# A decoder block's front half on one core: 64-row score blocks with a separate diagonal, a written order that reaches to the first pair's preparation, and the gate vector summed in idle buffers

## The chip, the core and the metric

The kernel runs on one core of a Trainium2 chip. The metric is the device time of one execution in microseconds (us). Times come from repeated executions, of which the median counts; the profile is of one further execution, with its own time.

## What is computed

A decoder block for 512 tokens of width 1024, depth 1. Window attention (8 heads of 64, window 128) and gated linear attention (4 heads, 64 keys by 128 values) share one input projection; the block ends with a layer of experts. Cut to what the change touches:

```python
mod = jax.nn.silu(c) @ w_ada[l] + b_ada[l]
shift1, scale1, gate1, shift2, scale2, gate2 = jnp.split(mod[:, None, :], 6, axis=-1)
h = rms_norm(x, norm1_w[l]) * (1.0 + scale1) + shift1
proj = h @ w_in[l]
aq, ak, av, gq, gk, gv, gg, glr = jnp.split(proj, split_points, axis=-1)
...
b = jnp.cumsum(gt, axis=2)
...
decay = jnp.exp(jnp.where(causal[:, :, None], diff, -jnp.inf))
att = jnp.einsum('bhtd,bhsd,bhtsd->bhts', qt, kt, decay)
...
mixed = jnp.concatenate([att, go], axis=-1) @ w_out[l]
x = x + gate1 * mixed
```

## The kernel before, in words

The tokens are four tiles of 128. The first fifth of the run, called the front half here, ends with the output projection and the second norm; after it comes the expert layer, which this change does not touch.

The front half has three stretches. **The quarter stage** (lines 354 to 443) runs in a fixed written order for all engines (`tc.manual_schedule`). The shift and scale vectors of the first norm are sums over `w_mod` weights, which DVE makes quarter by quarter (`quarter_sum`, L269 and L271); PE turns a quarter's sum into columns (`quarter_columns`, L278), DVE adds the bias (`quarter_rows`, L282 and L283), ACT writes two rows k of the normed input in a high part (`h_row`, L312) and DVE its low part (`h_low`, L317). Each k then feeds products into five PSUM banks at once (`first_products`, run at L348): the low-rank gate (`pglr`) and the column groups 3 and 4 of `w_in` (the queries and keys of the linear attention). Every matmul of the projections is three: high by high, high by low, low by high. The weights of groups 3 and 4 are split into a high part by ACT (L327) and a low part by GpSimd (L328), in halves `w3,0`, `w3,1`, `w4,0`, `w4,1`; the high and low parts live in rings of three buffers each, so `w4,1` takes the buffer of `w3,0`, which the products of k 0 to 3 read.

**The projections 0 to 2** (L70 to L72 into tiles named `pj`) follow: attention queries, keys, values. Beside them DVE and ACT work out the decays (`decays`) and the preparation of the first pair of token tiles (`gla_prep(0)`): prefix sums, eight differences `Eg[L]`, one absolute value over seven of them (L582) and one exponential over eight (L583) on ACT, and 14 products with q and k (L588, L589) plus one (L593) on DVE.

**The attention stretch** is all that follows up to the output projection `pw`: scores of the linear attention for four tiles (`gla_scores`, into PSUM `pa`), window attention for four tiles (`attention`: `sc`, the softmax on DVE and ACT in tiles `sS`, transposes `pt`, products `po`), the second pair's preparation, the value and gate projections 5 to 8 (`proj_N`, tiles `pn`), and the vectors 2, 3 and 4 of the modulation (`mod_part`): each loads eight 128x1024 blocks of `w_ada` (two per 1 MB transfer `wa`, L214) and sums them on DVE (`macc`, L218 and L220). These transfers share a ring of three 1 MB buffers ("raw") with the projections' weights (`wi`, L247) and the output projection's (`wo`, L770). Vector 2 is the gate `gate1b`; it is spread over the partitions by two matmuls with ones (L227, tiles `gb`) and added to its bias (L228). In this stretch the order on each engine is made by a scheduler from a model of the times, with the source order as the start.

`gla_scores` cuts the causal 128x128 block of a tile into levels: level 0 is the lower half by the upper half (L611), level 1 two 32x32 pieces (L614), levels 2 to 6 are made 32 rows at a time (L627, 32x16 each, of which a mask keeps a part, L634), and the block diagonal of 32x32 is a product of k and q without decay (L630, mask L637). That is 4 + 8 + 80 + 16 matmuls for a tile. ACT then copies the pieces into the tile `at` (three copies and four).

## Time and profile before

| | us |
|---|---|
| median of 3 runs | 1479.56 (1479.05 to 1480.74) |
| the profiled execution's own time | 1479.41 |
| its span | 1477.6 |
| busy in the span: PE / DVE / ACT / GpSimd | 1428.0 / 1279.9 / 680.3 / 557.5 |
| quarter stage ends, projections 0 to 2 end | 62.5, 97.7 |
| first matmul of the output projection | 228.3 |

All starts are counted from the start of the span. PE is TensorE, PEld its weight loads, DVE VectorE, ACT ScalarE, POOL GpSimd, SP the engine that issues most DMAs. A row of a timeline gives start, duration, engine, line, operation, output<-inputs, shape, count, and in brackets how long the engine was idle before it and who released it ("issue": nothing the profile shows). A row of the windows gives the stretch, its length, then for each engine the busy time and in parentheses the number of instructions, then the mean TensorE clock granted (1.00 is full), the share of the DMA engines and their rate. A matmul of plain fp32 (scores, transposes, sums) stands in the records as two, one of the projections' format (fp32r) as one.

### The profile page before, as it was taken

To read this page: it belongs to the slowest core of one execution; us is meant where nothing else is said; L and a number is where in the kernel's file an instruction comes from. 1 tells how busy PE (TensorE), PEld (TensorE's weight loads), DVE (VectorE), ACT (ScalarE), POOL (GpSimd) and SP (SyncE) were. 2 spreads that over 40 slices of the span, in tenths; PEclk is the share of its full clock that TensorE was granted. 3 is DMA by queue.
4 is the path that set the end of the run, shared out by engine and by line. 5 is a ranking of instruction groups with operands and counts; after the bars stand their busy time and mean duration, and the time that the engine had idled before them with its cause. 6 is when DMAs were issued, how large, how long until landed. Compare 5 with 4: busy or idle time off the path is not lost.

```text
span 1477.6 us, 24740 instructions
## 1 busy us (share of the span) xinstructions
PE 1428.0 (97%) x9427; PEld 1269.7 (86%) x9427; DVE 1279.9 (87%) x2475; ACT 680.3 (46%) x1073; POOL 557.5 (38%) x386
## 2 busy tenths in 40 slices
PE   4989899999999999999999999999999999999997
PEld 3778587788899999999999888888888888888886
DVE  7487647859999899999886998999999989999997
ACT  4545366643343365555765334333333334333334
POOL 4000000034441344421023666666666666544520
PEclk9999699999999999999999999999999999999999
DMA  9252605535246889997789999999999999999972
GB/s 358 102 187 90 224 30 199 177 126 205 73 156 228 321 301 343 338 364 267 255 292 383 414 412 414 412 414 402 383 405 394 398 405 410 410 411 413 410 301 72
DMA packets 130072, 439.57 MB, mean 297 GB/s; under 512 B 13328, under 2 KB 49440, under 8 KB 109600
## 3 DMA queue, kind: packets, MB, share of 16 engines
q1 hardware_dynamic: 71728, 258.42, 46.1%
q0 software_dynamic: 44832, 163.60, 28.5%
q10 hardware_dynamic: 13392, 15.97, 3.0%
q8 instruction: 74, 1.21, 0.3%
q14 instruction: 46, 0.38, 0.1%
HBM read 393.36 MB, written 44.52 MB: 296 GB/s over the span
## 4 chain that ended last, share of the span: by engine, by line
PE 82%; DVE 8%; DMA 4%; issue 3%; ACT 2%; POOL 0%; SPq 0%; ACTq 0%; DVEq 0%; POOLq 0%
PE acc L72 12%; PE acc L70 12%; PE acc L71 11%; PE ph L70 9%; PE ph L72 9%; PE ph L71 9%; PE pg L1080 4%; DMA Gd<-gs 1%; DMA wa<-in_w_ada_dram 1%; PE pj L348 1%; PE pn L70 1%; PE sc L526 1%; PE pn L71 1%; PE pn L72 1%; PE pw L71 1%
## 5 line engine op out<-in xcount | busy, mean ns | idle before, releaser
L1207 POOL DMA_INDIRECT gu<-in_u_dram,ix_u x128 | 194.4, 1519 | 193.6 <-PE pg L1080 77.8
L1242 POOL DMA_INDIRECT gv<-in_vP_dram,ix_v x128 | 196.8, 1537 | 155.0 <-DVE gu L1217 54.5
L841 ACT ACTIVATE ge<-ph 128x336 f32<-128x336 f32 x128 | 57.7, 451 | 309.2 <-PE ph L72 306.5
L1247 DVE SCALAR_TENSOR_TENSOR gacc<-gv,hg,gacc 128x1024 f32<-128x1024 f32 x127 | 162.2, 1277 | 5.0 <-DMA gv<-in_vP_dram,ix_v 4.7
L1217 DVE SCALAR_TENSOR_TENSOR gu<-gu,h2n 128x1024 f32<-128x1024 f32 x128 | 155.2, 1216 | 3.2 <-DMA gu<-in_u_dram,ix_u 3.1
L1155 POOL DMA_INDIRECT spr<-in_u_dram,spix x48 | 81.7, 1702 | 164.7 <-DVE spr L1161 124.1
L1525 ACT ACTIVATE Ah<-gr 128x384 fp32r<-128x384 f32 x128 | 66.6, 520 | 104.5 <-DVE gr L1522 104.0
L1301 POOL IOTA iot<- 128x256 bf16 x1 | 1.5, 1536 | 257.8 <-DVE h2Tl L816 257.8
L1082 ACT ACTIVATE gs<-pg 128x512 f32<-128x512 f32 x96 | 95.5, 1109 | 2.2 <-PE pg L1080 2.2
L1073 DVE TENSOR_TENSOR o<-o,gp 128x3072 bf16<-128x3072 bf16 x48 | 84.0, 1750 | 5.3 <-PE pg L1080 5.2
L1537 DVE TENSOR_TENSOR Al<-gr,Ah 128x384 fp32r<-128x384 f32 x128 | 70.3, 549 | 4.8 <-DMA Gd<-gs 4.8
L1080 PE MATMUL pg<-o,o 128*128 128x128 bf16 x1152 | 74.1, 219 | 0.0
L1080 PEld LDWEIGHTS <-o 128*128 128x128 bf16 x1152 | 66.9, 97 | 4.6
L1161 DVE SCALAR_TENSOR_TENSOR spr<-spr,xs 128x1024 f32<-128x1024 f32 x48 | 58.4, 1217 | 10.7 <-DMA spr<-in_u_dram,spix 10.7
L1055 DVE TENSOR_TENSOR o<-iot,t 128x2048 bf16<-128x2048 bf16 x48 | 58.2, 1218 | 6.0 <-PE pg L1080 4.1
L220 DVE SCALAR_TENSOR_TENSOR macc<-wa,scs,macc 128x1024 f32<-128x1024 f32 x28 | 38.4, 1372 | 5.0 <-DMA wa<-in_w_ada_dram 4.7
L1522 DVE TENSOR_TENSOR gr<-gel,gr 128x336 f32<-128x336 f32 x64 | 32.0, 501 | 0.0
L71 PE MATMUL pq<-h2Tl,wq_0h 128*128 128x512 f32 (+1 forms) x80 | 27.9, 349 | 1.2 <-DVE h2Tl L816 1.2
L70 PE MATMUL pq<-h2Th,wq_0h 128*128 128x512 f32 (+1 forms) x80 | 28.0, 352 | 1.0 <-ACT qsc L907 1.0
L72 PE MATMUL pq<-h2Th,wq_1l 128*128 128x512 f32 (+1 forms) x80 | 28.2, 353 | 0.0
L71 PE MATMUL pq<-h2Tl,wq_1h 128*128 128x512 f32 (+1 forms) x80 | 28.0, 350 | 0.0
L70 PE MATMUL pq<-h2Th,wq_1h 128*128 128x512 f32 (+1 forms) x80 | 27.9, 349 | 0.0
(2590 smaller groups left out, 5039.0 us busy)
## 6 DMA issues: line engine op xcount, KB each, us to landing
u<-in_uT_dram SPq DMA_DIRECT2D x64, 1024.0 KB
v<-in_vP_dram SPq DMA_DIRECT2D x64, 1024.0 KB
gr<-Gd SPq DMA_DIRECT2D x15, 1536.0 KB
Gd<-gs SPq DMA_DIRECT2D x10, 2048.0 KB
wa<-in_w_ada_dram SPq DMA_DIRECT2D x16, 1024.0 KB
gsp<-ge ACTq DMA_DIRECT2D x88, 168.0 KB
gel<-gsp SPq DMA_DIRECT2D x32, 336.0 KB
wo<-in_w_out_dram SPq DMA_DIRECT2D x8, 1024.0 KB
```

The costliest lines, as they stand in the source:

```text
L70: nc.tensor.matmul(acc, lh, rh, start=start, stop=False)
L71: nc.tensor.matmul(acc, lh, rl, start=False, stop=False)
L72: return nc.tensor.matmul(acc, ll, rh, start=False, stop=stop)
L1073: nc.vector.tensor_tensor(o2, o12[:, :, 1, None].to_broadcast([P, H, 3, P, 2]), gp3[:, g0:g0 + H, :, None].to_broadcast([P, H, 3, P, 2]), ...
L1080: nc.tensor.matmul(pt[:, i, :], o12[:, g, 0, :, r], o2[:, g, m, :, r], start=(m == 0), stop=(m == 2))
L1082: evict = nc.scalar.activation(gs[:, :, q % 2, :, t0 + 4 * f:t0 + 4 * f + 4].rearrange("p c i a -> p a c i"), pt.rearrange("p a (c i) -> p ...
L1155: nc.gpsimd.indirect_dma_start(out=sp[m], out_offset=None, in_=a["u"], in_offset=bass.IndirectOffsetOnAxis(ap=sp["ix", i][:, j:j + 1], axi ...
L1207: nc.gpsimd.indirect_dma_start(out=ur, out_offset=None, in_=a["u"], in_offset=bass.IndirectOffsetOnAxis(ap=ix_u[:, s:s + 1], axis=0))
L1217: nc.vector.scalar_tensor_tensor(ur, ur, 1.0, h2n, op0=OP.mult, op1=OP.mult, accum_out=hid[:, s:s + 1])
L1242: nc.gpsimd.indirect_dma_start(out=vr, out_offset=None, in_=a["vP"], in_offset=bass.IndirectOffsetOnAxis(ap=ix_v[:, s:s + 1], axis=0))
L1247: nc.vector.scalar_tensor_tensor(gacc, vr, hg[:, s:s + 1], gacc, op0=OP.mult, op1=OP.add)
L1537: nc.vector.tensor_tensor(grp(Al), A, grp(Ah), OP.subtract)
```

## The change

It has three parts.

1. *Scores.* Levels 1 to 6 are each made in two blocks of 64 rows (4 heads each, stationary 64x64, 32 columns), with level 0 as before: 52 matmuls for a tile. The diagonal is separate: GpSimd multiplies q by k into `Eg[NL + 1]`, PE sums it over the 64 rows of a head with a selection matrix `sel` (four matmuls into `pd` for a pair of tiles), DVE copies it out. The masked copies on DVE are six of 128x128 and one of 128x256 for a tile; ACT copies level 0 and two 64-row blocks.
2. *Written order.* The fixed order now reaches from the first quarter to the transposes of the values after projection 2; the decays, the projections 0 to 2 and the first pair's preparation are spelled out in it. Inside the quarter stage, the low parts of groups 3 and 4 move from GpSimd to DVE, the second half of group 3 is loaded behind the third quarter's weights, and group 4's products are run quarter by quarter instead of being kept for k 0 to 3 in one run behind `xt2`.
3. *Gate vector.* Its eight weight blocks are loaded one by one into tiles that are idle then (the softmax tiles, parts of `Eg` and `qT`), issued behind the weights of group 0, and summed on DVE at the end of the quarter stage and in projection 0; its two matmuls stand ahead of projection 1. The parts 3 and 4 stand in the source behind `proj_N(8)`.

The diff, cut to its core:

```diff
+    def mod_loads(k0, k1):
+        for k in range(k0, k1):
+            if k < 2:
+                home = frT.tile([P, 4, 256], F32, tag="sS", bufs=2, name=f"wm{k}")
+            else:
+                home = (Eg[:, 4:6, :], Eg[:, 7:9, :], qT[:, 0:2, :], qT[:, 2:4, :], Eg[:, 0:2, :], Eg[:, 2:4, :])[k - 2]
+            gate_in[k] = home.rearrange("p a b -> p (a b)")
+            nc.sync.dma_start(gate_in[k], a["w_ada"][k * P:(k + 1) * P, :D])
+
+    def mod_sums(k0, k1):
+        if k0 == 0:
+            gate_in["acc"] = frA.tile([P, D], F32, tag="m4", bufs=2, name="macc_g")
+        for k in range(k0, k1):
+            mod_sum(gate_in["acc"], gate_in.pop(k), k)
...
+    def prep_ends(i):
...
+        nc.vector.tensor_tensor(qe, Eg[:, NL + 1, :], q, OP.mult)
+        nc.vector.tensor_copy(el, grp(Eg[:, NL + 1, :], P)[:, :, P - 1])
+        nc.gpsimd.tensor_tensor(Eg[:, NL + 1, :], q, k, OP.mult)
...
+    def diagonal(i):
+        pb = bank(f"pd{i}")
+        for n in range(2):
+            for j in range(2):
+                nc.tensor.matmul(pb[:, 4 * n:4 * n + 4].rearrange("p (s j) -> p s j", j=2)[:, :, j],
+                                 Eg[:, NL + 1, n * 256 + j * P:n * 256 + (j + 1) * P], sel, start=True, stop=True)
+        pd = frG.tile([P, 2, 4], F32, tag="pd", bufs=2, name=f"pd{i}")
+        nc.vector.tensor_copy(pd.rearrange("p n h -> p (n h)"), pb[:, 0:8])
+        return pd
...
-    def w_split(g, s):
+    def w_high(g, s):
+        nc.scalar.activation(w34[g, s][0], wraw["wi", g][:, 4 * s:4 * s + 4, :], AF.Copy)
+
+    def w_low(g, s):
         h, l = w34[g, s]
-        w = wraw["wi", g][:, 4 * s:4 * s + 4, :]
-        nc.scalar.activation(h, w, AF.Copy)
-        nc.gpsimd.tensor_tensor(l, w, h, OP.subtract)
+        nc.vector.tensor_tensor(l, wraw["wi", g][:, 4 * s:4 * s + 4, :], h, OP.subtract)
 
...
         quarter_load(2)
+        w_load(3, 1)
         w_load(4, 1)
         nc.scalar.activation(wgh, wg, AF.Copy)
...
+            if q == 0:
+                nc.vector.tensor_tensor(wgl, wg, wgh, OP.subtract)
+                w_low(3, 0)
             quarter_rows(q)
-            if q == 1:
-                h_row(k0)
-                w_split(4, 0)
-                h_row(k1)
-            else:
-                h_row(k0)
-                h_row(k1)
+            if q == 3:
+                del mtb
+            h_row(k0)
+            h_row(k1)
             if q == 0:
-                w_split(3, 1)
-            j0, j1 = (first_products(k, [A] + B3 + (B4 if q > 1 else [])) for k in (k0, k1))
+                w_high(4, 0)
+            elif q == 1:
+                w_high(3, 1)
             if nxt < 4:
                 quarter_sum(nxt, (1, 2))
             h_low(k0)
             if nxt < 4:
                 quarter_sum(nxt, (3, 4))
             h_low(k1)
+            if q < 2:
+                w_low(*((4, 0), (3, 1))[q])
+            elif q == 3:
+                w_high(0, 0)
+                w_low(0, 0)
+                mod_sums(0, 2)
...
-            run(j0)
             if q == 0:
+                run(first_products(k0, [A] + B3))
                 xt_part(1, range(NT))
-                run(j1[:3])
+                run(first_products(k1, [A] + B3))
+                run(first_products(k0, B4))
                 quarter_columns(1)
-                run(j1[3:])
+                run(first_products(k1, B4))
...
-            elif q == 1:
-                run(j1)
+                continue
+            run(first_products(k0, [A] + B3 + B4))
+            if nxt < 4:
+                xt_part(nxt, range(NT))
+            jobs = first_products(k1, [A] + B3 + B4)
+            run(jobs[:6])
+            if nxt < 4:
+                quarter_columns(nxt)
+            run(jobs[6:])
+            jobs = None
+            if q == 1:
...
                 w_alloc(4, 1)
-                w_split(4, 1)
-                xt_part(2, range(NT))
-                for k in range(4):
-                    ops = B4
-                    run(first_products(k, ops))
-                    if k == 0:
-                        quarter_columns(2)
-                w34.pop((4, 0))
+                w_high(4, 1)
+                w_low(4, 1)
+                wraw.pop(("wi", 3))
+                mod_loads(0, 4)
+                fetch(a["w_in"][1], 1, 256, "wi")
+                mod_loads(4, 6)
...
+                wraw.pop(("wi", 4))
+                mod_loads(6, KD)
+                fetch(a["w_in"][2], 2, 256, "wi")
+                bcast_load(ba_tile(), a["b_ada"][0:1, 2 * D:3 * D], D)
...
+        w_high(0, 1)
+        mod_sums(2, 4)
+        w_low(0, 1)
+        mod_sums(4, 6)
+        pz = bank("pz0")
+        z_product(0, pz)
+        evict(p3.pop(), halves_of(gq, 1), 0.125)
+        pj = pbank("pj00")
+        group_products(0, 0, pj)
+        z_chain(0, pz)
+        evict(p3.pop(), halves_of(gq, 0), 0.125)
+        mod_sums(6, KD)
+        evict(pj, qT[:, 0, :], 0.125)
+        pz = bank("pz1")
+        z_product(1, pz)
+        pj = pbank("pj01")
+        group_products(0, 1, pj)
...
+        gate_products()
+        evict(pj, qT[:, 1, :], 0.125)
+        pj = pbank("pj10")
+        group_products(1, 0, pj)
+        prep_diffs(0)
+        gate_adds()
+        w_alloc(2, 0)
...
-        for L in (*LW, NL):
-            m = 64 >> L
-            for b0 in (0, 64):
+        for L in LW:
+            lo = 64 + (L - 1) * 32
+            for B in (0, 64):
                 for j, s, r, c in heads:
-                    for b in (b0, b0 + 32):
-                        cb = slice(c + b, c + b + 32)
-                        if L < NL:
-                            lo = 96 + (L - 2) * 16
-                            nc.tensor.matmul(pa[b:b + 32, 2 * s + j, lo:lo + 16], E[r, L, cb], late(E[r, L, cb], m),
-                                             start=True, stop=True)
-                        else:
-                            nc.tensor.matmul(pa[b:b + 32, 2 * s + j, 176:208], k[r, cb], q[r, cb], start=True, stop=True)
+                    cb = slice(c + B, c + B + 64)
+                    nc.tensor.matmul(pa[B:B + 64, 2 * s + j, lo:lo + 32], E[r, L, cb], late(E[r, L, cb], 64 >> L),
+                                     start=True, stop=True)
+        if n % 2 == 0:
...
+        nc.vector.copy_predicated(tc64, lm[:, NL - 1, :].bitcast(U16)[:, None].to_broadcast([P, 4, 64]),
+                                  pd[:, n % 2, :][:, :, None].to_broadcast([P, 4, 64]))
+        for b in (0, 64):
+            nc.scalar.activation(at[b:b + 64, :, b:b + 64], tc64[b:b + 64], AF.Copy)
...
     proj_N(5, gv, 0)
-    mod_part(2, frA, "m4", 2, dst=gate1b)
     attention(1)
     proj_N(6, gv, 256)
-    mod_part(3, frA, "m4", 2)
     gla_scores(2)
     gla_state(0, False)
     attention(2)
     gla_scores(3)
     gla_state(1, False)
     proj_N(7, gg, 0)
-    mod_part(4, frA, "m4", 2)
     attention(3)
     proj_N(8, gg, 256)
+    mod_part(3, frA, "m4", 2)
+    mod_part(4, frA, "m4", 2)
```

What moves on the engines follows in pieces of the instruction order. Line numbers are those of each kernel's own file; a number behind a name tells tiles of one name apart.

On ACT, at the turn from the second to the third quarter (`hTh`/`h32` are the rows from `xt1` and `xt2`, `wi3_1hi` and so on the high parts), before:

```order
L327 ACTIVATE wi4_0hi_281<-wi4_208 128x1024
L312 ACTIVATE hTh_182<-xt1_324,modT_83,aT_84 128x512
L312 ACTIVATE h32_3_368<-xt1_324,modT_83,aT_84 128x512
L327 ACTIVATE wi4_1hi_398<-wi4_208 128x1024
L312 ACTIVATE hTh_182<-xt2_402,modT_83,aT_84 128x512
```

and now:

```order
L429 ACTIVATE hTh_186<-xt1_328,modT_83,aT_84 128x512
L429 ACTIVATE h32_3_382<-xt1_328,modT_83,aT_84 128x512
L442 ACTIVATE wi3_1hi_284<-wi3_201 128x1024
L442 ACTIVATE wi4_1hi_439<-wi4_211 128x1024
L429 ACTIVATE hTh_186<-xt2_411,modT_83,aT_84 128x512
```

The high part of `w4,1` stands right ahead of the first row from `xt2` in both; the high part of `w3,1` has come in ahead of it, that of `w4,0` has left.

On DVE at the same place (`macc2`, `macc3` are the sums of the third and fourth quarter; `modT` and `aT` are what `h_row` of `xt2` reads), before:

```order
L271 SCALAR_TENSOR_TENSOR macc2_359<-mixA3_117,scs_85,macc2_359 128x512
L269 TENSOR_SCALAR macc3_439<-la0_103,scs_85 128x512
L282 TENSOR_TENSOR modT_83<-mt_187,vec_69 128x2x2
L283 SCALAR_TENSOR_TENSOR aT_84<-modT_83,vec_69 128x2
L271 SCALAR_TENSOR_TENSOR macc3_439<-gq0_104,scs_85,macc3_439 128x512
```

and now:

```order
L388 SCALAR_TENSOR_TENSOR macc2_375<-mixA3_117,scs_85,macc2_375 128x512
L446 TENSOR_TENSOR wi4_1lo_440<-wi4_211,wi4_1hi_439 128x1024
L386 TENSOR_SCALAR macc3_453<-la0_103,scs_85 128x512
L399 TENSOR_TENSOR modT_83<-mt_191,vec_69 128x2x2
L400 SCALAR_TENSOR_TENSOR aT_84<-modT_83,vec_69 128x2
L388 SCALAR_TENSOR_TENSOR macc3_453<-gq0_104,scs_85,macc3_453 128x512
```

The low part of `w4,1` now stands on DVE between the last sum of the third quarter and the rows `modT` and `aT`; before, it was on GpSimd.

On DVE in the attention stretch, around the masked copies of the third tile's scores (`macc4` and `macc3` are the sums of vectors 4 and 3, `wa4_4` and so on their transfers of two blocks, `wi7` and `wi8` the weights of projections 7 and 8, `mx` the softmax's maxima), before:

```order
L220 SCALAR_TENSOR_TENSOR macc4_2078<-wa4_6_2091,scs_85,macc4_2078 128x1024
L634 COPY_PREDICATED atc0_174<-lm_138,pa2_1536 128x16x4
L533 TENSOR_REDUCE mx20_1707<-sc200_1699 128x2
L220 SCALAR_TENSOR_TENSOR macc4_2078<-wa4_6_2091,scs_85,macc4_2078 128x1024
L634 COPY_PREDICATED atc0_174<-lm_138,pa2_1536 128x32x2
L533 TENSOR_REDUCE mx20_1707<-sc201_1700 128x2
L634 COPY_PREDICATED atc0_174<-lm_138,pa2_1536 128x64
L66 TENSOR_TENSOR wi8_0l_2213<-wi8_2210,wi8_0h_2212 128x1024
```

and now:

```order
L232 SCALAR_TENSOR_TENSOR macc3_2053<-wa3_2_2058,scs_85,macc3_2053 128x1024
L66 TENSOR_TENSOR wi7_1l_1732<-wi7_1725,wi7_1h_1731 128x1024
L232 SCALAR_TENSOR_TENSOR macc3_2053<-wa3_2_2058,scs_85,macc3_2053 128x1024
L66 TENSOR_TENSOR wi8_0l_1944<-wi8_1941,wi8_0h_1943 128x1024
L756 COPY_PREDICATED atc0_178<-lm_138,pa2_1406 128x4x32
L756 COPY_PREDICATED atc0_178<-lm_138,pa2_1406 128x8x16
L232 SCALAR_TENSOR_TENSOR macc3_2053<-wa3_4_2062,scs_85,macc3_2053 128x1024
L756 COPY_PREDICATED atc0_178<-lm_138,pa2_1406 128x16x8
```

Before, vector 4 is at its end here and vector 3 done; now vector 3 is in its first half, and the first low part of `wi8` has come ahead of the copies. Further on, from the last blocks of vector 4 to the second low part of `wi8`, now:

```order
L232 SCALAR_TENSOR_TENSOR macc4_2080<-wa4_6_2093,scs_85,macc4_2080 128x1024 x2
L756 COPY_PREDICATED atc1_179<-lm_138,pa3_1619 128x4x32
L706 TENSOR_TENSOR Z21_1578<-Z21_1578,es21_1579 128x4
L756 COPY_PREDICATED atc1_179<-lm_138,pa3_1619 128x8x16
L707 RECIPROCAL Z21_1578<-Z21_1578 128x4
L756 COPY_PREDICATED atc1_179<-lm_138,pa3_1619 128x16x8
L709 TENSOR_SCALAR sS21_1567<-sS21_1567,Z21_1578 128x256 x4
L756 COPY_PREDICATED atc1_179<-lm_138,pa3_1619 128x32x4
L756 COPY_PREDICATED atc1_179<-lm_138,pa3_1619 128x64x2
L756 COPY_PREDICATED atc1_179<-lm_138,pa3_1619 128x128
L759 COPY_PREDICATED atc1_179<-lm_138,pd1_1465 128x256
L66 TENSOR_TENSOR wi8_1l_1948<-wi8_1941,wi8_1h_1947 128x1024
```

The second low part of `wi8`, with which its raw buffer comes free, stands behind all sums of vectors 3 and 4.

From the first matmul of the expert layer (`pq`, at about 282 us before) to the end, the order on all five engines is the same in both kernels.

326 lines of the change are left out of this document (178 added, 148 removed).

## Prediction

> **What bounds the kernel now.** First the page: engine shares by slice, then the granted clock, then the chain of waits.
>
> ```profile
> PE   4989899999999999999999999999999999999997
> PEclk9999699999999999999999999999999999999999
> PE 82%; DVE 8%; DMA 4%; issue 3%; ACT 2%; POOL 0%; SPq 0%; ACTq 0%; DVEq 0%; POOLq 0%
> ```
>
> A slice is 37 us. PE is full nearly everywhere and carries 82% of the chain; its row falls below 9 only in the first five slices and the last, and the clock only in the fifth (148 to 185 us). These five are the front half, and only there does the instruction order change. From 282 us on the order is the same on every engine, so what the front gains or loses is carried to the end one for one. The windows show where the front loses time:
>
> ```profile
> 97.67:228.27 130.60, 117.29 (x1581) 96.77 (x1580) 82.98 (x203) 65.62 (x177) 0.00 (x0) 0.88 0.36 122
> 136.88:188.40 51.52, 43.78 (x640) 33.87 (x638) 38.53 (x86) 20.70 (x69) 0.00 (x0) 0.77 0.55 189
> 62.48:97.67 35.19, 35.19 (x150) 27.47 (x149) 25.90 (x46) 23.58 (x31) 0.00 (x0) 1.00 0.38 135
> ```
>
> The first number behind the length is PE's busy time, the third DVE's; behind ACT's and POOL's stands the clock. The projections (last row) are bound by PE with no gap. The attention stretch (first row) takes 130.6 us, of which PE is idle 130.60 - 117.29 = 13.3 us, and 12% of the busy time, 14.1 us, is lost to a slow clock: 27.4 us together. Its middle (second row) has DVE busy for 38.5 of 51.5 us. Where the clock falls:
>
> ```profile
> 100.00:105.00 5.00, 3.69 (x203) 3.11 (x202) 3.58 (x4) 0.60 (x1) 0.00 (x0) 1.00 0.96 373
> 105.00:110.00 5.00, 2.14 (x11) 1.63 (x11) 2.33 (x5) 1.06 (x1) 0.00 (x0) 0.64 0.73 254
> 110.00:115.00 5.00, 5.00 (x31) 4.96 (x31) 3.45 (x15) 3.08 (x14) 0.00 (x0) 0.67 0.62 211
> 150.00:155.00 5.00, 4.85 (x150) 3.79 (x149) 4.58 (x10) 4.32 (x11) 0.00 (x0) 0.66 0.83 259
> 160.00:165.00 5.00, 5.00 (x26) 3.59 (x25) 3.63 (x5) 0.00 (x0) 0.00 (x0) 0.55 1.01 360
> ```
>
> PE's waits from 97 to 229 us (total, times, longest), then two of those from 0 to 63 us:
>
> ```profile
> PE pa L630 <- issue: 5.2, 2, 4.2
> ...
> PE pglr L348 <- DVE hTl L317: 2.1, 2, 1.8
> PE mt L278 <- DVE macc L271: 2.0, 2, 1.4
> ```
>
> The longest, 4.2 us, lies in the first tile's scores, in a burst of tiny matmuls; nothing the profile shows releases it, and the DMA engines are at 0.96 there. I read it as instructions that arrive late.
>
> **The quarter stage.** The waits for `hTl` and `macc` come from this:
>
> ```profile
> 28.61 0.48 DVE L269 TENSOR_SCALAR macc<-qT,scs 128x512 f32<-128x512 f32 x1
> 29.84 0.16 DVE L282 TENSOR_TENSOR modT<-mt,vec 128x4 f32<-128x4 f32 x1 [0.75 <-PE mt L278]
> 30.29 0.78 ACT L312 ACTIVATE hTh<-xt,modT,aT 128x512 fp32r<-128x512 f32 x1 [5.90 <-DVE aT L283]
> 32.38 0.75 DVE L271 SCALAR_TENSOR_TENSOR macc<-qT,scs,macc 128x512 f32<-128x512 f32 x1
> 32.76 2.61 POOL L328 TENSOR_TENSOR wi_0lo<-wi,wi_0hi 128x1024 fp32r<-128x1024 f32 x1 [5.40 <-ACT wi_0hi L327]
> 33.16 2.76 DVE L271 SCALAR_TENSOR_TENSOR macc<-mixA,scs,macc 128x512 f32<-128x512 f32 x1
> 37.52 1.06 ACT L327 ACTIVATE wi_1hi<-wi 128x1024 fp32r<-128x1024 f32 x1 [3.50 <-issue]
> ```
>
> A sum takes DVE 0.75 us alone and 2.76 beside GpSimd's subtraction of 2.61. With the subtractions on DVE these stretched rows go, and with them the two waits, 2.1 + 2.0 = 4.1 us. Against that stands a new wait. The high part of `w4,1` waits for PE's last product of k 3 from the ring buffer it takes over, and the first row of `xt2` stands behind it on ACT and, through `modT` and `aT`, behind its low part on DVE. Before, 16 products of group 4 covered this; now six are left behind that last read. The chain is 1.06 (high part) + 1.22 (low part, row `wi_0l` below) + 0.48 (first sum) + 2 x 0.16 + 0.78 (row of h) = 3.9 us, and about 0.1 at each of five handovers, 4.4; six products at 0.23 us, read off the projections (150 records in 35.19 us), cover 1.4. So PE idles 3.0 us. Net -1.1. A gap of that size may cost clock: from nothing to 5 x 0.33 = 1.7 us, by the windows at 0.67; I take 0.6. **Sum -0.5** (-1.1 to +1.2).
>
> [...]
>
> **The gate vector.** These groups are of the stretch from 97 us on:
>
> ```profile
> L220 DVE SCALAR_TENSOR_TENSOR macc<-wa,scs,macc 128x1024 f32<-128x1024 f32 x19 | 24.3, 1279 | 2.4 <-DMA wa<-in_w_ada_dram 2.1
> L66 DVE TENSOR_TENSOR wi_0l<-wi,wi_0h 128x1024 fp32r<-128x1024 f32 x3 | 3.7, 1220 | 0.0
> L634 DVE COPY_PREDICATED atc<-lm,pa 128x64 f32<-128x64 uint16 x20 | 5.1, 253 | 4.1 <-PE pa L630 3.9
> L637 DVE COPY_PREDICATED atc<-lm,pa 128x128 f32<-128x128 uint16 x4 | 1.2, 300 | 0.1
> L227 PE MATMUL gb<-macc,ones 128*128 128x512 f32 x4 | 2.3, 644 | 0.0
> ```
>
> Its eight sums, 8 x 1.28 = 10.2 us, move to the end of the quarter stage and into projection 0, where DVE has 35.2 - 25.9 = 9.3 us free in the projections alone and no row of PE waits on it; hidden. Were that cover gone, up to 1 us would show. Its two matmuls add up to 2.3 us to the PE-bound projections: **+2.1**. They leave the attention stretch, where they stand beside the softmax of tile 1 and bring little back.
>
> **The scores.** The burst in the first tile, and how long tiny matmuls take:
>
> ```profile
> 97.67 0.45 PE L611 MATMUL pa<-Eg 64*64 64x64 f32 x8
> 98.04 0.34 PE L614 MATMUL pa<-Eg 64*32 64x32 f32 x16
> 98.54 0.28 PE L71 MATMUL pn<-wi_0l,hTh 128*128 128x256 f32 x1
> 98.66 0.28 PE L72 MATMUL pn<-wi_0h,hTl 128*128 128x256 f32 x1
> 101.91 1.50 PE L627 MATMUL pa<-Eg 64*32 64x16 f32 x158
> 103.28 0.41 PE L630 MATMUL pa<-gq,gk 64*32 64x32 f32 x25
> ```
>
> Before, a tile costs 0.45 + 0.34 + 1.50 + 0.41 = 2.7 us. The new form, 96 records of 64x64 by 32, is not in this trace. Its bounds are the 64x32 row, 0.34 / 16 = 0.021, and the 64x64 by 64 row, 0.45 / 8 = 0.056 us: 2.0 to 5.4 us. I take 0.03, since the moving size is that of the first: 2.9, and 0.45 for level 0 and 0.5 for half a diagonal (eight records, at most pn's spacing of 0.12), 3.8. So +1.1 a tile (+0.2 to +3.6). The matmuls get dearer, yet fewer: 104 records a tile in place of 216 (a matmul of these stands as two), half of the burst; the 4.2 us wait and the slow clock behind it, 2.14 x 0.36 + 5.0 x 0.33 = 2.4 us, should go. On DVE the copies become 6 x 0.30 and one of 128x256, at 0.42: 2.2 in place of 1.6 us a tile, +0.6.
>
> **To the second pair's products.** The end of tile 1's scores and the products behind it:
>
> ```profile
> 125.41 0.44 PE L630 MATMUL pa<-gq,gk 64*32 64x32 f32 x28
> 136.88 0.42 DVE L588 TENSOR_TENSOR Eg<-Eg,gq 128x256 f32<-128x256 f32 x1
> ```
>
> From 97.67 to 125.85 PE loses the wait (4.2), the slow clock (2.4), 30 of 72 `pn` matmuls that now stand later (30 x 0.12 = 3.6), and four transposes and four products of attention 0 (at `pn`'s spacing 1.0): 11.2. It gains two tiles' scores (2.2), and the values' transposes come up to 0.9 later, since a high part of 1.06 us stands ahead of their eviction on ACT. Net -8.1. From there to the products took 11.0 us; about 1.8 of it (a high part, two small copies) leaves ACT's queue. With -0.5 and +2.1 before it, the products start 0.5 - 2.1 + 8.1 + 1.8 = **8.3 us earlier**.
>
> GpSimd's new product of q and k (128x512) runs beside DVE here. By the 2.61 and 2.76 rows it may stretch one DVE row by half of 2.0, 1.0 us a pair; it stands beside the 3.6 us and more that ACT needs for `Eg`, and I count nothing. [...]
>
> **The softmax stretch.** From there to the last softmax of tile 2:
>
> ```profile
> 160.98 0.34 SPq L247 DMA_DIRECT2D wi<-in_w_in_dram  x1
> 168.24 1.06 ACT L65 ACTIVATE wi_0h<-wi 128x1024 fp32r<-128x1024 f32 x1 [9.94 <-DMA wi<-in_w_in_dram]
> 187.25 1.14 DVE L543 TENSOR_SCALAR sS<-sS,Z 128x256 f32<-128x256 f32 x4
> 228.27 0.73 PE L70 MATMUL pw<-wo0000h,ah 128*128 128x512 f32 x2
> ```
>
> It took 51.5 us with DVE busy 38.5. Now DVE has more to do in it: the low part of `wi6` (1.2), one more sum (1.3), the third and fourth tiles' copies (0.6 + 2.2), tile 0's state output (about 2, worked out as four rows of the size of the `sS` rows and small ones), another low part of `mixA` (0.7): +8.0, 46.5 us. Its idle time, 13.0, falls where the sums now stand between the steps of a softmax, but the transfers of vectors 3 and 4 now go through one or two raw buffers, since `wi7` and `wi8` hold theirs till late: I take 8 (4 to 13). 54.5, **+3.0** (-1 to +8).
>
> **The rest.** From 188.4 to 228.3 PE was nearly full. 58 `pn` matmuls have moved ahead of it: -6.9; some of them covered waits for the last softmax and for `wo`, so I take **-5.4** (-6.9 to -3).
>
> **Sum.** -8.3 + 3.0 - 5.4 = -10.7, from the profiled execution's own 1479.41 (span 1477.6 and 1.8 around it): 1468.7. The median stands 0.15 above the profile: **1468.9 us**.
>
> **The rivals.**
>
> *Slower: the transfers line up.* If `wi8`'s buffer, free only behind the last sum, leaves vectors 3 and 4 one buffer, each transfer must land (168.24 - 160.98 = 7.3 us) before its two sums (2.5), 9.8 us for each of eight: 78 us for the softmax stretch in place of 51.5, and -8.3 + 26.9 - 5.4 = +13: 1492.6. It decides from (51.5 + 8.3 + 5.4) / 8 = 8.2 us a transfer. For it: 9.94 us of ACT waiting for `wi`. Against: that transfer shared the DMA with two others (share 1.01), and `wi7` frees a second buffer after two transfers. 0.11.
>
> *No change: a slow clock eats the lead.* PE's work in the stretch is 43.78 x 0.77 = 33.7 us at full clock. With `pn` matmuls taken out it has less to bridge the gaps; at 0.55, as at 160 us, it would need 61.3, +9.8, and half of the last term would go too (+2.7): -8.3 + 9.8 - 2.7 = -1.2, 1478.2. For it: 0.55 to 0.66 with little idle time. 0.12.
>
> *The burst still starves.* 104 records may outrun the instruction supply as well, with `wi8`'s transfer landing at the same moment: 4.2 + 2.4 come back, 1475.3. For it: a second wait of 1.0 at the same line, without DMA traffic to blame. Against: the 24 slow products of projection 2 stand right ahead of it now. 0.10.
>
> *More: the clock stays full.* Of the 27.4 us lost, only 6 remain: -21.4, 1458.0. It needs a softmax stretch bound by PE, which DVE's 46.5 us speak against. 0.12.
>
> **How the numbers follow.** My own sum has 0.55, with ends at about 1462 and 1476 by the bounds above. The range, 1458 to 1479, takes in the starving burst, the slow clock and the edge of the full clock, and leaves out the lined-up transfers and some of the ends. A measurement of this kernel tells about 0.2%, 3 us, from no change. Faster by more: 0.55 + 0.10 + 0.12 less 0.01 for the sum's upper end, 0.76. Within: 0.12 + 0.01, 0.13. Slower: 0.11.
>
> **What would show it.** GpSimd's subtractions and the 2.76 us rows gone; PE idle about 3 us ahead of k 4, at 42 to 45 us; projections ending near 99; no wait "issue" at the scores, or one under 1 us; the second pair's products starting near 128.6; the last `sS` of tile 2 near 183; `pw` near 217.6. It is wrong if DVE's waits for `wa` exceed 8 us, if the clock row of the fifth slice stays at 6, or if a part behind 282 us changes its length.

## The result and the profile after

The changed kernel takes 1470.72 us, the median of four runs (1468.47 to 1472.3); the kernel before took 1479.88 beside it. The ratio is 0.9937 with a 95% interval of 0.992 to 0.9954: 9.2 us faster, where 10.7 were forecast. The profiled execution of the changed kernel took 1472.3 (span 1470.5) and is the slowest of its four, so the traces show 7.1 us of the 9.2. In the experiments two single executions, of 2743.5 and 2027.1 us, were disturbed and are left out.

The page of the changed kernel: PE by slice, the granted clock by slice, the chain.

```profile
PE   5998999899999999999999999999999999999997
PEclk9999999999999999999999999999999999999999
PE 84%; DVE 8%; ACT 3%; DMA 3%; issue 1%; POOL 1%; SPq 0%; ACTq 0%; POOLq 0%; DVEq 0%
```

The 6 in the clock's fifth slice is gone and "issue" falls from 3% to 1% of the chain. Now windows of the changed kernel, in the order of the program: projections 0 to 2; the softmax stretch from the second pair's products to the last `sS` of tile 2; from there to the first `pw`; from there to the last `pw`; and last, all from the projections' end to the last `pw`. (Length, then PE, weight loads, DVE, ACT and GpSimd with their counts, the clock, the DMA share and rate.)

```profile
63.33:100.80 37.47, 37.47 (x161) 28.45 (x160) 31.75 (x48) 23.27 (x32) 1.55 (x1) 1.00 0.25 85
127.11:184.37 57.26, 54.19 (x561) 45.49 (x561) 45.67 (x104) 25.92 (x77) 0.00 (x0) 0.97 0.51 168
184.37:215.80 31.43, 29.95 (x236) 26.15 (x235) 17.11 (x51) 24.27 (x55) 0.00 (x0) 0.95 0.20 65
215.80:275.20 59.40, 56.13 (x287) 44.35 (x286) 45.45 (x81) 34.11 (x65) 0.00 (x0) 1.00 0.58 196
100.80:275.20 174.40, 162.56 (x1409) 134.86 (x1409) 125.39 (x283) 100.00 (x227) 1.29 (x1) 0.98 0.42 140
```

The same two last stretches of the kernel before, the longer one first:

```profile
97.57:282.14 184.57, 170.44 (x1849) 139.98 (x1848) 127.27 (x282) 100.93 (x241) 0.00 (x0) 0.92 0.44 152
228.27:282.14 53.87, 53.05 (x270) 43.20 (x268) 44.19 (x80) 35.31 (x65) 0.00 (x0) 1.00 0.65 226
```

Two sums can be made of these rows. The first goes by the prediction's steps:

| step | forecast, us | measured, us |
|---|---|---|
| quarter stage, end | -0.5 | +0.9 (62.48 to 63.33) |
| projections 0 to 2 | +2.1 | +2.4 (35.09 to 37.47) |
| second pair's products start, with both rows above | -8.3 | -9.8 (136.88 to 127.11) |
| softmax stretch | +3.0 | +5.7 (51.52 to 57.26) |
| from there to the first `pw` | -5.4 | -8.4 (39.87 to 31.43) |
| first to last `pw` | 0 | **+5.5** (53.87 to 59.40) |
| all behind it | 0 | -0.2 |
| span | -10.7 | -7.1 |

The second needs no landmark inside the stretch. From the projections' end to the last `pw` a length is PE's idle time, the part of its busy time lost to the clock, and the rest, which is PE's work at full clock. Before: 184.57 - 170.44 = 14.1 idle, 170.44 x 0.08 = 13.6 lost, 156.8 of work. After: 11.8 idle, 162.56 x 0.02 = 3.3 lost, 159.3. (The clock has two digits, so the last two are good to 0.8. The projections' end is taken 0.1 us earlier here than in the prediction's windows.) So of the 10.2 us that this stretch gains, the clock gives 10.3, idle time 2.3, and the rest takes 2.5. The prediction had booked 2.4 for the clock.

What PE waits for from 97 to 275 us in the changed kernel (total, times, longest):

```profile
PE pn L70 <- ACT gv L672: 4.0, 1, 4.0
PE po L724 <- ACT PT L719: 2.2, 2, 1.5
PE po L724 <- DVE gv L802: 1.6, 1, 1.6
PE pw L70 <- DVE mg L890: 1.2, 2, 0.8
```

The wait "issue" at the scores is gone, but a wait of 4.0 has come that no step foresaw. ACT's timeline shows where from:

```profile
119.52 3.20 ACT L324 ACTIVATE Eg<-Eg 128x3584 f32<-128x3584 f32 x1 [0.92 <-DVE Eg L309]
122.62 0.82 ACT L762 ACTIVATE at<-atc 64x256 f32<-64x256 f32 x2
123.46 3.62 ACT L327 ACTIVATE Eg<-Eg 128x4096 f32<-128x4096 f32 x1
126.99 0.37 ACT L672 ACTIVATE gv<-pn 128x256 f32<-128x256 f32 x1
```

The eviction of projection 5 (last row) stands behind the second pair's absolute value and exponential on ACT, and PE needs the bank it frees.

### The profile page after: what moved, and what is told of

The parts are those of the page before. It is cut to its first block, busy times and chain, and to the rows that moved or that the text cites. A ratio compares the mean times of both kernels' runs of the same rounds, so it can differ in the third digit from the quotient of the medians.

```text
span 1470.5 us, 23890 instructions
## 1 busy us (share of the span) xinstructions
PE 1424.0 (97%) x8995; PEld 1267.8 (86%) x8995; DVE 1286.1 (87%) x2488; ACT 680.4 (46%) x1059; POOL 548.6 (37%) x384
## 4 chain that ended last, share of the span: by engine, by line
PE 84%; DVE 8%; ACT 3%; DMA 3%; issue 1%; POOL 1%; SPq 0%; ACTq 0%; POOLq 0%; DVEq 0%
PE acc L72 12%; PE acc L70 12%; PE acc L71 12%; PE ph L72 10%; PE ph L70 10%; PE ph L71 10%; PE pg L1191 4%; DMA wa<-in_w_ada_dram 2%; DVE macc L232 1%; PE pj L466 1%; PE pw L70 1%; PE pw L72 1%; PE pw L71 1%; PE pj L70 1%; PE pj L71 1%
## 5 line engine op out<-in xcount | busy, mean ns | idle before, releaser
L232 DVE SCALAR_TENSOR_TENSOR macc<-wa,scs,macc 128x1024 f32<-128x1024 f32 x21 | 30.7, 1461 | 7.0 <-DMA wa<-in_w_ada_dram 6.8
L72 PE MATMUL pq<-h2Th,wq_0l 128*128 128x512 f32 (+1 forms) x80 | 28.3, 353 | 0.0
```

The source lines that it names most:

```text
L72: return nc.tensor.matmul(acc, ll, rh, start=False, stop=stop)
```

## The experiments

The question after the result was where the gain comes from. One reading is the prediction's: each part has a price at its place, the sums are added. The rival is that a part acts through the schedule of the whole attention stretch: which small matmuls come to stand together, how long PE is idle between them, and what clock it then gets. The runs take the parts one by one.

**The scores alone.** The kernel before with the first part of the change only:

```diff
-    LW = range(2, NL)
+    LW = range(1, NL)
...
-    atc = [frG.tile([P, 4, 32], F32, name=f"atc{i}") for i in range(2)]
+    atc = [frG.tile([P, 4, 64], F32, name=f"atc{i}") for i in range(2)]
...
+        nc.gpsimd.tensor_tensor(E[:, NL + 1, :], q, k, OP.mult)
```

> The kernel before with the 64-row scores and the separate diagonal alone; written order and gate vector as before. Theory A (the 4.2 us wait comes of the number of tiny matmuls in one burst): with 104 records a tile in place of 216 the wait 'issue' falls under 1 us, the slow clock behind it goes, and the time is 3 to 7 us under before, 1473 to 1477. Theory B (the wait comes of the transfers of vector 2 that land beside the burst, DMA share 0.96): the wait stays at 3 us or more and the time is within 3 us of before.

Measured: 1466.26 (1464.83 to 1470.91), ratio 0.991 (0.9893 to 0.9927). That is 13.7 us, more than the whole change. From the projections' end to the last `pw`, and, in the timeline, the first tile's levels 1 to 6:

```profile
98.55:268.72 170.17, 165.48 (x1417) 138.28 (x1416) 131.37 (x290) 96.41 (x225) 2.20 (x1) 0.95 0.48 165
```

```profile
102.00 1.62 PE L633 MATMUL pa<-Eg 64*64 64x32 f32 x96
```

The new burst runs through without a wait. PE is idle 4.7 us there where it was 14.1, and loses 8.3 to the clock where it lost 13.6; the work, 157.2, is that of before. So the wait goes, as Theory A had it, but the gain is about twice the most that it expected. Alone, the first part gives more than the whole change; the other two together cost 4.5 us beside it (4.0 by the ratios).

**Everything but the scores.** The changed kernel with the scores in 32-row pieces, as before:

```diff
-    LW = range(1, NL)
+    LW = range(2, NL)
...
-        if n % 2 == 0:
-            pds[n // 2] = diagonal(n // 2)
+        q, k, E = flat(gq[n // 2]), flat(gk[n // 2]), Eg
```

> The changed kernel with the 32-row scores back; written order and gate vector as changed. Theory A (number of tiny matmuls): the wait 'issue' at the first tile's scores is back with 1 to 4 us, and the time is 3 to 6 us over the changed kernel, 1474 to 1477. Theory B (transfers beside the burst): the DMA is nearly idle there now (share under 0.3), so no wait over 0.5 us, and the time is within 2 us of the changed kernel.

Measured: 1472.2 (1471.04 to 1472.96), ratio 0.9941 (0.9926 to 0.9956). That is 1.5 us above the changed kernel, which the intervals don't tell apart. The other two parts alone are worth 7.7 us; with the scores' 13.7 the sum would be 21.4, and the whole change gives 9.2. The parts do not add: beside the other two, the scores bring little. The wait came back as Theory A said, the 3 to 6 us did not. With the old scores the burst stops again, in a place where almost no transfer is under way. Two rows of PE's timeline and the window with its DMA share (0.03):

```profile
106.55 0.29 PE L755 MATMUL pa<-gq,gk 64*32 64x32 f32 x12
108.76 0.33 PE L755 MATMUL pa<-gq,gk 64*32 64x32 f32 x17 [1.92 <-issue]
```

```profile
105.00:110.00 5.00, 3.08 (x198) 2.49 (x198) 0.75 (x3) 0.00 (x0) 0.00 (x0) 0.97 0.03 7
```

**The scores issued twice.** The kernel with the scores alone, in which each matmul of levels 1 to 6 is issued two times in a row into the same place:

```diff
-                    nc.tensor.matmul(pa[B:B + 64, 2 * s + j, lo:lo + 32], E[r, L, cb], late(E[r, L, cb], 64 >> L),
-                                     start=True, stop=True)
+                    for again in range(2):
+                        nc.tensor.matmul(pa[B:B + 64, 2 * s + j, lo:lo + 32], E[r, L, cb], late(E[r, L, cb], 64 >> L),
+                                         start=True, stop=True)
```

> The kernel before with the 64-row scores alone, and each of the 48 matmuls of levels 1 to 6 issued twice, 192 records in a burst in place of 96, with the order ahead of it unchanged. Theory A (the number of records in a burst makes PE wait for instructions): a wait 'issue' of 1 to 4 us in the first tile's burst, slow clock behind it, and 8 to 14 us over the run with the scores alone (4 x 1.6 us of matmuls, the wait and the clock). Theory B (the 32-row form itself, with its 32-column stationary, makes the wait): no wait over 0.3 us, and 3 to 7 us over that run.

Measured: one run of 1477.93, span 1476.1, which is 12.5 above the scores alone. Most of that is the added work, as the table below shows. The burst itself does not stop; a wait of 1.03 us begins 1.5 us behind its end:

```profile
102.00 3.68 PE L634 MATMUL pa<-Eg 64*64 64x32 f32 x192
...
108.24 0.28 PE L71 MATMUL pn<-wi_1l,hTh 128*128 128x256 f32 x1 [1.03 <-issue]
```

192 records of the new form at 19 ns each lead to 1.03 us of waiting, 96 at 17 ns to none, so with the form kept, twice the number brings a wait. No slow clock follows it: the next slow stretch, at 113.6 us, stands in the trace of the scores alone as well. The old form ran its first 158 records in 1.50 us, 9.5 ns each, and waited 4.2 some 30 records later. A like number of records in half the time waits longer, which speaks for the number of records per time, but the form differs too. Whether traffic lengthens the wait is not shown: the old burst waited 1.92 us with the DMA at 0.03 and 4.2 with it at 0.96, but what stands ahead of it differs as well, and no run changes the traffic alone.

**The gate vector's place.** The changed kernel with the gate vector summed from the ring of raw buffers, as before:

```diff
-        gate_products()
-        gate_adds()
...
     proj_N(5, gv, 0)
+    mod_part(2, frA, "m4", 2, dst=gate1b)
```

> The changed kernel with the gate vector made as before: four transfers through the raw ring and eight sums in the attention stretch, its two matmuls out of the projections. Theory A (DVE and the ring bound the softmax stretch): projections 2.3 us shorter, but 10.2 us of sums and four transfers more in the attention stretch, so 4 to 10 us over the changed kernel, 1475 to 1481. Theory B (DVE has room there, 40% idle before the softmax stretch): within 2 us of the changed kernel.

Measured: 1470.39 (1468.95 to 1471.15), ratio 0.9928 (0.9913 to 0.9944). Its place is worth nothing that can be told, as Theory B had it. With the gate from the ring the projections take 35.7 us (64.54 to 100.25) in place of 37.5, so the place costs 1.8 there; the attention stretch, which then has the eight sums to make, is no longer for it (173.3 in place of 174.4).

**The vectors 3 and 4 early.** The changed kernel with them at the source places of before:

```diff
     proj_N(6, gv, 256)
+    mod_part(3, frA, "m4", 2)
...
     proj_N(7, gg, 0)
+    mod_part(4, frA, "m4", 2)
...
-    mod_part(3, frA, "m4", 2)
-    mod_part(4, frA, "m4", 2)
```

> The changed kernel with one thing undone: vectors 3 and 4 stand in the source where they stood before (behind the projections 6 and 7), not at the end. Theory A (their late place makes the order in which attention 3 and the states fall behind the output projection's start, 5.3 us more in the output stage than before): the output stage, from the first to the last pw matmul, falls from 59.4 to about 54 us, and the time is 3 to 5 us under the changed kernel, 1466 to 1468. Theory B (the loss is of the order ahead of it, which the written front sets): the output stage stays at 58 us or more and the time is within 1.5 us of the changed kernel.

Measured: 1478.69 (1471.17 to 1484.43, 12 runs), ratio 0.9982 (0.9968 to 0.9996): 8 us slower than the changed kernel (7 by the ratios), most of the gain, where neither theory expected a loss. The output stage came down by 3.2 to 56.2 us, and the time rose all the same. PE is idle less than in the changed kernel, 7.1 us, but loses 17.4 to the clock. A window of it, the one behind it, and what PE runs in the first (first three groups: output<-inputs, shape, count, busy time, mean ns):

```profile
157.62:181.51 23.89, 23.89 (x165) 15.69 (x161) 7.47 (x25) 9.13 (x35) 0.00 (x0) 0.50 0.11 39
181.51:184.92 3.41, 3.41 (x42) 3.37 (x39) 2.89 (x13) 0.31 (x2) 0.00 (x0) 0.98 0.00 0
```

```profile
L692 PE MATMUL sc<-kT,qT 64*128 64x256 f32 x16 | 8.3, 669 | 0.0
L748 PE MATMUL pa<-Eg 64*64 64x32 f32 x92 | 4.9, 295 | 0.0
L724 PE MATMUL po<-PT,vN 128*64 128x128 f32 x24 | 3.1, 405 | 0.0
```

PE is busy all 23.89 us, at half clock throughout. It runs almost only small matmuls of the attention and the scores; the `pn` matmuls, which stand between them elsewhere, are three records here. The next stretch of `pn` matmuls runs at the full clock. They did not bring it back, though: it returns at 181.5, behind small matmuls alone, and the first of them starts after that:

```profile
181.13 0.74 PE L748 MATMUL pa<-Eg 64*64 64x32 f32 x20
181.81 0.39 PE L70 MATMUL pn<-wi_0h,hTh 128*128 128x256 f32 x1
```

The slow clock isn't the same in every execution of this kernel, although the order of its instructions is. By the mean clock of a whole execution, three of the twelve had 0.991 to 0.993 and took 1471.2 to 1475.4 us; nine had 0.981 to 0.984 and took 1477.2 to 1484.4. So the order alone doesn't fix the clock, and a loss to the clock read from one trace is that of one execution.

**A cover for the wait ahead of k 4.** The changed kernel with group 4's products of k 2 and k 3 behind group 3's of both:

```diff
+            if q == 1:
+                run(first_products(k0, [A] + B3))
+                xt_part(nxt, range(NT))
+                run(first_products(k1, [A] + B3))
+                run(first_products(k0, B4))
+                quarter_columns(nxt)
+                run(first_products(k1, B4))
```

> The changed kernel with one thing turned in the quarter stage: group 4's products of k 2 and 3 stand behind group 3's of both, so 12 matmuls and the eight columns cover the high and low part of w4,1. Theory A (the wait ahead of k 4 and the slow clock behind it are real losses on PE's path): the wait of 2.6 us falls under 0.8, no window of 0.66 behind it, the projections end 3 to 4 us earlier, and the time is 2 to 4 us under the changed kernel, 1467 to 1469. Theory B (the lead is lost again in the softmax and output stages): the projections end 3 to 4 us earlier but the time is within 1.5 us of the changed kernel.

Measured: 1464.6 (1462.59 to 1466.01), ratio 0.989 (0.9871 to 0.9909): 6 us better than the changed kernel, more than either theory expected, and the best of all. The wait ahead of k 4 is gone and the quarter stage ends at 60.27 in place of 63.33. Of the 7.8 us by which its span is shorter (1462.7), 3.1 come from there; the other 4.7 come from the stretch behind the projections, which no edit touched: idle 5.9 in place of 11.8, clock 6.6 in place of 3.3, work 2.0 less. So the 4.7 come with another order in that stretch and are no price of the wait.

**The cover with the vectors early, and with the gate from the ring as well.** The diffs are those above, put together.

> The cover of the quarter stage (group 4's products of k 2 and 3 behind group 3's) and the early place of vectors 3 and 4 together, on the changed kernel. Theory A (both are separate losses on PE's path): their gains add, 6 from the cover and 3 to 5 more, 1459.5 to 1462. Theory B (the stretch behind gives the second back): within 1.5 us of the cover alone, 1463 to 1466.

> As the run with cover and early place, and the gate vector too through the raw ring as before: what is left of the change is the 64-row scores, the written order and the cover. Theory A (the gate's place is worth nothing, as the run that undid it alone showed): within 1.5 us of the run with cover and early place. Theory B (with the sums of vectors 3 and 4 early, DVE and the ring are full there, so that the gate's ten us of sums show): 3 to 6 us above it.

Measured: 1471.3 (1469.13 to 1475.08), ratio 0.9932 (0.9917 to 0.9948), and 1468.64 (1468.22 to 1470.49), ratio 0.9913 (0.99 to 0.9926). The early vectors again cost, 6.7 us this time, where the expectation had a gain or nothing. So, beside the other parts, their late place, for which the prediction had no term of its own, is part of the gain; with the scores alone, where they stand early too, the kernel takes 1466.3. The gate from the ring is again no loss: 2.7 us less, inside the intervals.

**Work in the wait.** The changed kernel with nine matmuls that nothing reads, ahead of k 4:

```diff
+            if q == 1:
+                for _ in range(9):
+                    nc.tensor.matmul(pgf[64:].rearrange('p (a w) -> p a w', a=2), identb[:, :64],
+                                     am[:, None, :].to_broadcast([P, 2, 256]), start=True, stop=True)
```

> The changed kernel with nine additional matmuls between the last products of k 3 and the first of k 4 (bfloat16, stationary 128x64, 512 columns, into 64 partitions of the gate's bank that nothing reads): some 2.1 us of work in the 2.6 us in which PE waits for the row of h. Everything else, the order on every engine too, is as in the changed kernel. If the wait costs its 2.6 us and, through an idle PE, another 1.5 us of slow clock behind it (the clock of 0.66 from 45 to 50 us), the wait stays in length, the clock stays at 1.00, the quarter stage ends about 1.5 us earlier (61.8 in place of 63.3) and the time falls by 1.5 us to about 1469.2. If the slow clock does not come from this wait, the stage ends at 63.3 as before, and the time stays at 1470.7. If the additional matmuls are themselves in the way, it is slower by up to 0.5 us.

> The same kernel as the one with nine additional matmuls ahead of k 4, for one more profile, since the first was of a disturbed run. If the slow clock comes from PE standing idle for 2.6 us, the window from 45 to 50 us stays at 1.00 and the quarter stage ends near 61.8. If it does not, the window shows 0.66 again or the slow stretch stands elsewhere, and the stage ends at 63.3.

The wait, and the same two windows of 3.41 us in the changed kernel and in this one:

```profile
45.23 0.40 PE L466 MATMUL pglr<-hTh,wgh 128*16 128x512 f32 x1 [2.58 <-ACT hTh L429]
```

```profile
42.05:45.46 3.41, 0.83 (x4) 0.29 (x3) 2.91 (x6) 1.45 (x3) 0.00 (x0) 1.00 1.03 423
45.46:48.87 3.41, 3.41 (x10) 2.43 (x9) 3.31 (x6) 1.73 (x3) 0.00 (x0) 0.51 0.98 396
```

```profile
42.05:45.46 3.41, 2.90 (x14) 1.28 (x13) 2.76 (x6) 1.45 (x3) 0.00 (x0) 1.00 1.03 420
45.46:48.87 3.41, 3.41 (x15) 2.50 (x16) 3.31 (x6) 1.88 (x3) 0.00 (x0) 1.00 0.99 407
```

With PE busy in the first window, the second has the full clock. The stage, from the first product of `pglr` to its end, takes 61.96 - 21.87 = 40.09 us in place of 63.33 - 21.54 = 41.79: 1.70 less, which is half of 3.41, though the nine matmuls compute nothing that is used. So in this pair of traces the idle time caused the slow clock. The other traces bear it out: in all five kernels that have this wait (the changed one, all but the scores, gate from the ring, vectors early, `gv` on DVE) it is 2.5 to 2.6 us long and one slow stretch of 3.41 us stands behind it; the four with the cover and this one have none in the stage. The time does not tell it: 1470.6 (1469.22 to 1473.5), ratio 0.993 (0.9914 to 0.9945), is 1.0 us better by the ratios, inside the interval; the second, single run took 1467.55 beside 1481.76.

**Projection 5's first evictions on DVE.** Meant to take the wait of 4.0 us for `gv` away, in the changed kernel and in that with the cover:

```diff
+                if g == 5 and n == 0:
+                    nc.vector.tensor_copy(dst[n + s][:, col:col + 256], pt[:, s, :])
+                else:
                     nc.scalar.activation(dst[n + s][:, col:col + 256], pt[:, s, :], AF.Copy)
```

> The changed kernel with the first two evictions of projection 5 on DVE in place of ACT, where they stood behind the absolute value (3.20 us) and the exponential (3.62 us) of the second pair and PE waited 3.99 us for them. The scheduler makes the order of the attention stretch anew from there. If that wait is a loss of its own, the front half ends about 4 us earlier (last product of the output projection near 271 in place of 275) and the time is about 1466.7. If PE's wait only takes the place of one that would stand elsewhere, since DVE sets this stretch, the wait for gv goes, others come, and the time stays at 1470.7.

> The changed kernel with both: group 4's products of k 2 and k 3 behind group 3's of both, which covered the wait ahead of k 4, and the first two evictions of projection 5 on DVE. With the cover alone the wait for gv was 1.34 us. If the two add up: 1464.7 - 1.3 = 1463.4. If DVE sets the stretch: 1464.7 or, with two more rows on DVE, 1465.4.

Measured: 1475.69 (1471.48 to 1477.02), ratio 0.9959 (0.9943 to 0.9975), and 1471.4 (1469.47 to 1472.11), ratio 0.9935 (0.9917 to 0.9952): 5 and 7 us worse than without the edit (3 and 7 by the ratios, of which the 3 is not clear of the noise), where a gain of 4 and of 1, or about none, was expected. In the first a wait of 2.9 us for `gv` remained, so it does not settle what that wait is worth. In the second it is gone:

```profile
97.60:272.59 174.99, 168.73 (x1405) 140.49 (x1404) 124.04 (x284) 99.40 (x225) 1.33 (x1) 0.93 0.41 142
```

PE is idle 6.3 us, as with the cover alone (5.9), but 168.73 x 0.07 = 11.8 go to the clock in place of 6.6: that is the loss in this trace.

All kernels in one table, each from the projections' end to the last `pw` of its own trace, in us:

| kernel | stretch | PE idle | lost to the clock | work at full clock | median time |
|---|---|---|---|---|---|
| before | 184.6 | 14.1 | 13.6 | 156.8 | 1479.9 |
| changed | 174.4 | 11.8 | 3.3 | 159.3 | 1470.7 |
| scores alone | 170.2 | 4.7 | 8.3 | 157.2 | 1466.3 |
| all but the scores | 174.0 | 8.4 | 9.9 | 155.7 | 1472.2 |
| gate from the ring | 173.3 | 7.7 | 5.0 | 160.7 | 1470.4 |
| vectors 3, 4 early | 181.4 | 7.1 | 17.4 | 156.9 | 1478.7 |
| cover | 169.7 | 5.9 | 6.6 | 157.3 | 1464.6 |
| cover, early | 179.7 | 11.9 | 10.1 | 157.8 | 1471.3 |
| cover, early, ring | 177.9 | 11.3 | 8.3 | 158.2 | 1468.6 |
| `gv` on DVE | 176.2 | 10.9 | 8.3 | 157.0 | 1475.7 |
| cover, `gv` on DVE | 175.0 | 6.3 | 11.8 | 156.9 | 1471.4 |
| work in the wait | 172.5 | 10.8 | 3.2 | 158.5 | 1470.6 |
| scores issued twice | 184.0 | 9.6 | 5.2 | 169.2 | 1477.9 (one run) |

But for the doubled scores the work hardly moves: 156 to 161. What differs is idle time and clock. By the traces, PE's order in this stretch is another one in every kernel except the one with work in the wait, whose order is that of the changed kernel, and there alone both stay as they were (10.8 and 3.2 beside 11.8 and 3.3).

## Why the prediction was right, and where it was not

The time was right and so was the sign, but four terms were off and partly made up for each other, so that the nearness of the number is partly luck.

*Quarter stage.* Both waits went, with the rows at 2.76. The first line is of the groups of the changed kernel from 21 to 63 us, the second the only one that PE's waits have there:

```profile
L388 DVE SCALAR_TENSOR_TENSOR macc<-mixA,scs,macc 128x512 f32<-128x512 f32 x4 | 3.0, 750 | 0.1
```

```profile
PE pglr L466 <- ACT hTh L429: 3.9, 2, 2.6
```

A sum of 128x512 takes 0.75 us in every group there, and of the two waits the longer is the new one ahead of k 4, 2.58 us (forecast 3.0). The first product came 0.5 later, at 21.54 in place of 21.07; the start varies between the traces, from 21.07 to 21.99 where the stage's order is that of before. From there on the stage took 41.79 in place of 41.41, +0.4. Without the slow clock it takes 40.09, 1.3 less than before, by the run with work in the wait; the prediction said 1.1. The clock was mis-sized: 1.7, the end of its range, where 0.6 was taken. The slow clock doesn't need the new wait, though: in the two other traces with the stage of before (scores alone, scores issued twice) a slow stretch of 3.41 us stands at 31.7 us, and the trace of before happened to have none there. In the changed kernel 2.58 us of idle time, with PE busy for 0.83 of the 3.41 us ahead of the slow stretch, were enough. The prediction's 0.1 for a handover between engines was an estimate that no run shows; in this chain the changed kernel has 0.04 from the high part's end on ACT (42.44 us) to the low part on DVE, 0.03 from `aT`'s end on DVE (44.37) to the row of h on ACT, and 0.05 from its end (45.18) to PE.

*Projections and gate vector.* +2.4 for +2.1, and PE shows no wait for the sums; 1.8 of it is the gate's, by the run with the gate from the ring.

*Scores.* The price was too high. The first tile in the changed kernel:

```profile
100.90 1.16 PE L748 MATMUL pa<-Eg 64*64 64x32 f32 x64
...
102.96 0.69 PE L748 MATMUL pa<-Eg 64*64 64x32 f32 x32
103.58 1.05 PE L342 MATMUL pd<-sel,Eg 128*128 128x2 f32 x8
```

A record takes (1.16 + 0.69) / 96 = 0.019 us, below both bounds (0.021 and 0.056) and below the 0.03 taken. A tile with its level 0 and half a diagonal costs 0.45 + 1.85 + 0.53 = 2.8 and not 3.8: the same as before. PE has no wait "issue" from 97 to 275 us, so the rival "the burst still starves" is out; in the single run with doubled matmuls a wait of 1.03 us came behind 192 records of this form.

*GpSimd's products.* Each, 1.55 us from 86.35 and 1.29 from 106.37 us on, ran beside a longer row of DVE: a scan of 0.67 us took 1.72 (at 86.73 us) and a masked copy of 0.45 took 1.27 (at 106.69). That is 1.05 and 0.82, near the 1.0 of the prediction's estimate, and no wait of PE comes of it, so counting nothing held.

*Softmax stretch.* +5.7 for +3.0. DVE is busy 45.67 us there, as forecast (46.5), and the transfers cost it 5.6 us of waiting in five waits, not the 78 us stretch of the rival "the transfers line up". But DVE's time was the wrong thing to add up. PE is busy 54.19 of the 57.26 us, and its work at full clock there is 54.19 x 0.97 = 52.6 us in place of 43.78 x 0.77 = 33.7: with the `pn` matmuls taken in, the stretch is PE's. With the vectors early again DVE is busy for only 27.9 us there, the stretch is down to 44.8, and the kernel is slower all the same. Why a whole order comes out faster or slower is read from PE's idle time and clock.

*The failed step: nothing between the first `pw` and the end.* The sum treated the start of `pw` as if all that precedes it in time were done. In the changed kernel the first `pw` stands ahead of more of attention 3's transposes and products: from there to the last `pw` PE is busy 56.13 us in place of 53.05, and idle 3.3 in place of 0.8, with waits for `mg`, `gh` and a low part of `wo`. Whether the late vectors bring this order about stays open: with the cover the output stage takes 57.8 us with them late and 58.0 with them early. So 5.5 of the 12.5 us that `pw` came earlier were given back. From the last `pw` on the lead does hold, -6.9 there and -7.1 at the end. The term "the rest" and this one belong together: -8.4 + 5.5 = -2.9, where -5.4 stood.

*The clock.* It was booked as a consequence of the starving burst (2.4) and as a rival each way. It is the largest term: 10.3 us, as much as the stretch behind the projections gains in all (10.2). The mechanism of the rival "a slow clock eats the lead" is real, and the run with the vectors early shows it at its full size (17.4); the change happens to stand on its good side. Of the rival "the clock stays full" the clock came nearly true, the gain did not, since idle time stayed at 11.8. For the gap ahead of k 4 a run shows why the clock falls; why a given order of the stretch behind gets the clock it gets is not shown, since no run was made for it, and what the traces have stands below.

## What to carry to other kernels

Where PE does the same work in every version, add up its idle time and the clock it loses over the whole stretch, and take a landmark such as a first matmul only when nothing older is left behind it. Here a wait of 2.6 us cost 1.7 more behind it: filling it with idle work gave the 1.7 back, covering it with useful work made the stage 3.2 shorter (60.27 - 21.71 = 38.56 us in place of 41.79). Parts that pass through one scheduler don't add, so time each alone: here one part alone beat all three by 4.5 us. And an edit in one place can move what the scheduler does in another: of the 7.8 us that the cover gave by the traces, 4.7 came from a stretch that it did not touch.

## What the runs showed of the hardware

*Clock.* In the 13 traces used here the granted clock was 0.5 or 1.0 and changed on a grid of 3.41 us. In the first 300 us they have 42 slow stretches, each 3.41 us long or a multiple of it, up to 23.89. Of these, 30 follow a window with 0 to 2.6 us of work in 3.41; yet such a window isn't always followed by one (1.62 us of work in the 3.41 from 34.76 us on in the kernel before, clock 1.00 in the next). The other 12 follow a window that was full (3.41 us of work). In six of those full windows, one each of the kernel before, the changed one, that with the vectors early and the cover alone, and two of the cover with `gv` on DVE, sums of `macc`, scores or transposes take the most time (1.9 us are sums of `macc` in that of the kernel before, 2.7 in that of the changed one). Three windows of the changed kernel:

```profile
202.47:205.88 3.41, 3.41 (x34) 3.41 (x33) 2.68 (x7) 3.27 (x12) 0.00 (x0) 1.00 0.00 0
205.88:209.29 3.41, 3.41 (x19) 3.41 (x17) 0.94 (x7) 2.92 (x5) 0.00 (x0) 0.51 0.00 0
209.29:212.70 3.41, 3.41 (x34) 3.07 (x33) 1.79 (x5) 2.16 (x3) 0.00 (x0) 0.99 0.02 5
```

The largest group of PE in the first of them:

```profile
L223 PE MATMUL mt<-ones,macc 128*128 128x1 f32 x24 | 2.7, 247 | 0.0
```

The first window holds mostly such sums of `macc` into one column, the second mostly `pn` matmuls, behind which the clock returns. With the 23.89 us at 0.50 above, it looks as if what PE runs counts, not whether the page calls it busy; against it stands the return at 181.5 there, behind small matmuls alone. No run changes the kind of matmul alone, so which of them holds is not shown.

*Bursts of tiny matmuls.* The old burst stopped for 4.2 us with the DMA at 0.96 (kernel before) and for 1.92 us with it at 0.03 (all but the scores). Of the new form PE got through 96 records at 17 ns each without a wait (scores alone), and into one of 1.03 us behind 192 at 19 ns (scores issued twice, one run). The profile puts these waits down to nothing ("issue"); that instructions arrive late is a reading of them.
